# States times C in a two-branch block: decays put on C, channel-major by head pairs; output weights split earlier

## The chip, the cores and the metric

One core of a Trainium2 chip runs the whole kernel. The metric is device microseconds of one execution, as the median of 3 runs. TensorE (PE) multiplies into PSUM; its weight loads (PEld) are a queue of their own. VectorE (DVE), ScalarE (ACT) and GpSimd (POOL) work elementwise, each in the order of its own queue. SyncE (SP) and ACT issue the DMAs.

## What is computed

A block over 2048 latent tokens of 1024 channels (and 256 context tokens) has one input projection that feeds two mixers: box means on a grid, and a state-space scan in both directions with 16 heads of 64 channels in 4 groups. The scan goes in chunks of 128 tokens. For a chunk the output of a head is

```
y_diag = (C B^T masked, times decay) applied to x
y_off  = einsum('bclgn,bcgrpn,bclgr->bclgrp', C, h_start, exp(acum))
y      = y_diag + y_off          # forward, and the same backward; + d_skip * x
```

so `y_off` is the state at the chunk's border times C, scaled for each token and head by the exponential of the decay sum. y is gated, normed by group, joined with the pooled branch and multiplied by `w_out` (2048 x 1024); the kernel scales the rows of `w_out` (by `pool_scale` or the norm's weight) and its columns (by the gate `g_l`) once, ahead of time. Then come the residual and a last norm.

## The kernel before, in words

Channels lie on the partitions nearly everywhere. A projection's operands are split into a rounded part and a rest (`hi`, `lo`: a copy on ACT, a subtraction on POOL or DVE), and three matmuls of 512 columns make one product. The stages:

- **Convolution stage** (loop over 16 column tiles `ct`, lines 576 to 596). For each tile 4 blocks of 512 tokens are projected; for `ct` < 12 also the 256 context tokens (`hc`). A block's result is copied out of PSUM by ACT, goes through a convolution of three `scalar_tensor_tensor` on DVE (line 270) between two ACT operations, and is stored. Tiles 0 and 1 were spilled before; their convolutions (`recall`, the list `late`) come in blocks of `ct` 13 to 15. `gate_row` sums the gate row in `ct` 10 to 13 and stores it.
- **Upper projections** (lines 710 to 754): the upper half of the tokens through the gates and the pool branch, with the backward scan of states (`sweep`) between the matmuls. Here 8 of the 16 tiles of `w_out` are loaded, scaled (`rescale`, DVE reading the gate from two PSUM buffers `gb`) and stored to `s_wo`.
- **Lower projections and boxes** (lines 756 to 871): the lower half, and the box sums on DVE. `prepare(0)` to `prepare(3)` load a tile of `w_out`, scale it, copy the rounded part (ACT) and subtract the rest (POOL or DVE, line 851).
- **Ramp** (`RAMP`, lines 1207 to 1228): an order written out by hand for the first four steps, the last gate projections and `prepare(5)` to `prepare(8)`; `prepare(9)` to `(15)` follow.
- **Steps** (lines 1235 to 1253): 64 steps, one for each chunk c and group g of 4 heads. Every engine gets the operations of `ORDER` in that order; the number beside a name says which step it works on (-1 is the next step, 1 the one before). `carried` (line 911) multiplies C by both states (tokens on partitions, PSUM tile `yo`); `from_states` (line 941) scales the result by `ee_t` into `yt` on DVE; `outputs` (line 968) transposes the skip part and both halves of `yt` into PSUM tile `y` and adds the diagonal part, four matmuls of 64 output rows, the two heads of a pair on the two halves of the rows. `gate` (DVE) reads `y`. `state` (line 948) moves the forward state on, on POOL. `exponents`, `mix`, `mix2` (DVE), `shift`, `steps_mix`, `decay` (ACT) build the diagonal factor `m`; `norm1`, `norm2`, `diag`, `spread`, `scale` are the norm; `pool_lo`, `ssd_lo` are POOL's subtractions (line 960); `out` is the output product, 24 matmuls a step; `f0` to `f9` are the end of a chunk, spread over five steps.

Outside `RAMP` and the steps the framework orders each engine's queue itself. `aux` and `pp` are four PSUM buffers each.

Of the kernel before, what the change touches and what calls it, by code (L numbers as in the profile page):

```python
# [23 lines left out]
def hybrid_block(ctx, tc, d, out):  # L24
# [40 lines left out]
    s_gate = dram("s_gate", [P, 1024])  # L65
    s_wo = dram("s_wo", [8, P, 1024])
# [267 lines left out]
    wd = dp.tile([P, 8, P], F32R, tag="wd", name="wd")  # L334
# [168 lines left out]
    triL = const("triL", [P, P], d["triL"], pool=tabs)  # L503
    n4 = [P, 2, NC2, 16]
# [57 lines left out]
    def gate_row(k):  # L562

        wg = rpool.tile([P, 1024], F32, tag="wraw", name=f"wg{k}")
        nc.sync.dma_start(wg, d["w_ada"][k * P:(k + 1) * P, 2048:3072])
        if k == 0:
            nc.vector.tensor_scalar(gacc, wg, scol[:, k, 0:1], None, op0=ALU.mult)
        else:
            nc.vector.scalar_tensor_tensor(gacc, wg, scol[:, k, 0:1], gacc, op0=ALU.mult, op1=ALU.add)
        if k == 7:  # L570
            brow = rpool.tile([1, 1024], F32, tag="wraw", name="brow")
            nc.sync.dma_start(brow, d["b_g"])
            nc.vector.tensor_tensor(gacc[0:1, :], gacc[0:1, :], brow, op=ALU.add)
            nc.scalar.dma_start(s_gate, gacc)
# [4 lines left out]
    for ct in range(2, 16):  # L579
# [130 lines left out]
    with tc.tile_pool(name="sweepp", bufs=2) as bp, tc.tile_pool(name="evp", bufs=3) as ep:  # L710
# [10 lines left out]
        def rescale(raw, k):  # L721

            for j in range(2):
                js = raw[:, 512 * j:512 * j + 512]
                nc.vector.scalar_tensor_tensor(js, js, rowscale[:, k:k + 1], gb[j], op0=ALU.mult, op1=ALU.mult)

        upper = (2, 3)
        for j in range(8):
# [118 lines left out]

    def prep_lo(k, eng=None):
        wo = wout[k // 4][:, k % 4]
        eng = eng or (nc.gpsimd if k in (1,3,4,5,7,13,15) else nc.vector)  # L850
        eng.tensor_tensor(wo[:, 1, :], raws[k], wo[:, 0, :].bitcast(F32), op=ALU.subtract)  # L851

    def prepare(k):
        prep_load(k)
        prep_scale(k)
        prep_hi(k)
        prep_lo(k)
# [15 lines left out]
    class Step:  # L873
# [27 lines left out]

        def shift(s):
# [7 lines left out]

        def carried(s):

            g = s.g
            s.po = aux(f"yo{s.nm}")
            mm(s.po[:, 0:256], s.bc[:, 1, :], hst[:, g], True, True)
            mm(s.po[:, 256:512], s.bc[:, 1, :], s.st[:, 1, :], True, True)
# [210 lines left out]
    def z_tail(ps, j, b):  # L1127
# [12 lines left out]
        ("shift", -1, ('shift',)),  # L1140
# [10 lines left out]
        ("state", 0, ('state',)),  # L1151
        ("mask", -1, ('mask',)),
        ("outputs", 0, ('outputs',)),
        ("exponents", -1, ('exponents',)),
        ("steps_mix", -1, ('steps_mix',)),
        ("out01", 2, ('out', 0, 1)),
        ("decay", -1, ('decay',)),
        ("carried", -1, ('carried',)),
        ("f2", 0, None),
        ("pool_hi", 0, ('pool_hi',)),  # L1160
        ("gate", 0, ('gate',)),
        ("mix", -1, ('mix',)),
# [3 lines left out]
        ("squares", 0, ('squares',)),  # L1166
        ("square_sum", 0, ('square_sum',)),
# [35 lines left out]
    other = {f.__name__: f for f in (prep_load, prep_scale, prep_hi, prep_lo, z, zg, logs, work, more)}  # L1203
# [4 lines left out]
    0:load prep_load/5 1:load 0:scores 0:carried 0:shift 0:mask 0:exponents prep_scale/5 1:shift 0:steps_mix  # L1208
    prep_hi/5 logs 0:decay z/6/0 1:scores 1:carried zg/6/0 z/7/0 0:mix 0:from_states prep_load/6 
    0:mix2 1:mask 1:exponents 2:load prep_scale/6 1:steps_mix prep_hi/6 1:decay zg/7/0 2:scores 2:carried more  # L1210
    1:from_states 1:mix 0:outputs z/6/1 prep_lo/5 prep_load/7 0:load_pool prep_lo/6
    0:gate 2:mask prep_scale/7 1:mix2 prep_load/8 1:load_pool 0:squares 2:shift
    2:steps_mix 0:square_sum 2:exponents 1:outputs 0:norm_mm z/7/1 more work prep_hi/8 prep_hi/7 zg/6/1 prep_lo/8
    0:state prep_lo/7 3:load 2:from_states 1:gate 0:pool_hi 1:squares zg/7/1 logs 0:norm1 
    1:square_sum 0:norm2/0 1:pool_hi 2:decay 2:mix 0:pool_lo 1:pool_lo 3:scores 1:norm_mm 0:out/0/0
    0:out/0/1 1:norm1 0:norm2/1 0:norm2/2 0:norm2/3 0:diag 0:spread 2:mix2 3:mask 2:outputs 1:out/0/0 0:scale 3:carried 1:out/0/1
    0:ssd_hi 3:shift 2:state 0:ssd_lo 1:state 2:gate 3:steps_mix 2:squares 2:square_sum 3:exponents 2:norm_mm
    1:norm2/0
# [98 lines left out]
```

## Time and profile before

| | |
|---|---|
| median of 3 runs | 1695.05 us (1692.56 to 1697.28) |
| profiled execution | 1691.25 us; its span 1689.5 us |
| mean granted clock of TensorE | 0.983 |
| busy share of the span | PE 96%, PEld 77%, DVE 72%, ACT 45%, POOL 35% |
| HBM read, written | 207.28 MB, 93.62 MB |

The stages end at about 491 us (convolution), 823 (upper), 1057 (lower), 1154 (ramp), 1662 (steps). A line of a group reads: line of the kernel, engine, operation, out<-in, shapes, count | busy us, mean ns of one | idle time of the engine just before them, and who ended it. A matmul of plain 32-bit floats is two instructions in the trace. An instruction's time counts from when its engine took it up, so that it holds what it waits for inside the engine.

### The profile page before, as it was taken

The numbers are of one execution on the slowest core, as the hardware profiler recorded it, in microseconds if no ns is written. First come the engines' busy times: TensorE is split into PE (matmuls) and PEld (weight loads), VectorE is DVE, ScalarE is ACT, GpSimd is POOL, SyncE is SP. The second block draws the span as 40 slices with busy tenths as digits, with TensorE's granted clock in tenths as the row PEclk, the third lists the DMA queues.
The fourth block names the chain that finished last, engine by engine and source line by source line (L and its number), as shares of the span: only waits on it lengthen the run. The fifth ranks groups of instructions, "written<-read, shape, count | busy, mean of one in ns | idle before, by whom it ended". The sixth has DMA issues, their size and how long they took to land. (4 is left out here: it accounts for less than half of the span.)

```text
span 1689.5 us, 25001 instructions
## 1 busy us (share of the span) xinstructions
PE 1626.3 (96%) x7786; PEld 1306.6 (77%) x7786; DVE 1209.4 (72%) x2514; ACT 768.4 (45%) x1841; POOL 599.5 (35%) x667
## 2 busy tenths in 40 slices
PE   8889999999999999999999989869999999999997
PEld 6668888888887887787887868757888888888886
DVE  2575755566772888886199998547788888888885
ACT  5563453433453444443212122455565556555653
POOL 1231111111223667775433334323333333333331
PEclk9989999999999999999999999989999999999999
DMA  9823333466564678878624356675666667666762
GB/s 388 283 75 100 76 74 73 93 155 155 144 137 153 203 248 252 255 249 272 207 87 150 114 184 187 188 223 184 186 194 208 195 203 199 198 208 192 194 194 83
DMA packets 315543, 302.57 MB, mean 179 GB/s; under 512 B 132626, under 2 KB 244114, under 8 KB 312851
## 3 DMA queue, kind: packets, MB, share of 16 engines
q1 hardware_dynamic: 246594, 237.27, 48.9%
q10 hardware_dynamic: 68816, 63.71, 11.3%
q8 instruction: 61, 1.00, 0.2%
q14 instruction: 72, 0.58, 0.1%
HBM read 207.28 MB, written 93.62 MB: 178 GB/s over the span
## 5 line engine op out<-in xcount | busy, mean ns | idle before, releaser
L52 PE MATMUL px<-hm,w_x 128*128 128x512 f32 x1536 | 364.8, 397 | 2.7 <-ACT hm L205 2.4
L52 PEld LDWEIGHTS px<-hm,w_x 128*128 128x128 f32 x1536 | 288.0, 188 | 73.3 <-ACT hm L205 4.1
L52 PE MATMUL po<-wout,yp 128*128 128x512 f32 x768 | 213.0, 413 | 0.0
L52 PE MATMUL po<-wout,ys 128*128 128x512 f32 x768 | 211.0, 410 | 0.0
L52 PE MATMUL pz<-hm,w_z 128*128 128x512 f32 x768 | 188.9, 398 | 0.7 <-POOL w_z L220 0.7
L270 DVE SCALAR_TENSOR_TENSOR cacc<-u,conv_w,cacc 128x512 f32<-128x512 f32 x168 | 141.5, 854 | 66.3 <-POOL u L320 47.5
L52 PEld LDWEIGHTS pz<-hm,w_z 128*128 128x128 f32 x768 | 145.0, 189 | 36.0 <-POOL w_z L220 1.1
L52 PEld LDWEIGHTS po<-wout,yp 128*128 128x128 f32 x768 | 135.9, 190 | 34.7 <-issue 10.6
L52 PEld LDWEIGHTS po<-wout,ys 128*128 128x128 f32 x768 | 136.3, 190 | 23.7
L960 POOL TENSOR_TENSOR yp<-yl,yp 128x256 fp32r<-128x256 f32 x64 | 50.3, 786 | 229.2 <-ACT yp L956 220.8
L644 DVE TENSOR_TENSOR xw<-xt,w_t 128x256 f32<-128x256 f32 x144 | 99.3, 728 | 31.5 <-POOL xr L651 17.0
L651 POOL TENSOR_TENSOR xr<-xw,xh 128x512 fp32r<-128x512 f32 x72 | 99.7, 1387 | 27.4 <-ACT xh L649 27.4
L960 POOL TENSOR_TENSOR ys<-yg,ys 128x256 fp32r<-128x256 f32 x64 | 63.1, 986 | 116.9 <-ACT ys L956 66.6
L52 PE MATMUL ivationFunctionType.Copy<-hm,ivationFunctionType.Copy 128*128 128x512 f32 x384 | 97.7, 401 | 2.3 <-POOL ivationFunctionType.Copy L220 1.7
L52 PE MATMUL pv<-hm,w_v 128*128 128x512 f32 x384 | 92.9, 402 | 5.9 <-ACT zt L795 5.9
L52 PE MATMUL ivationFunctionType.Silu<-hm,ivationFunctionType.Silu 128*128 128x512 f32 x384 | 95.9, 396 | 0.0
L649 ACT CAST xh<-xw 128x512 fp32r<-128x512 f32 x72 | 44.7, 621 | 110.0 <-DVE xw L644 48.9
L52 PE MATMUL pzp<-hm,w_q 128*128 128x512 f32 x384 | 91.3, 396 | 1.2 <-ACT va L788 1.2
L52 PEld LDWEIGHTS pv<-hm,w_v 128*128 128x128 f32 x384 | 73.6, 192 | 24.1 <-ACT zt L795 6.3
L52 PEld LDWEIGHTS ivationFunctionType.Copy<-hm,ivationFunctionType.Copy 128*128 128x128 f32 x384 | 73.1, 191 | 20.5 <-POOL ivationFunctionType.Copy L220 2.1
L52 PEld LDWEIGHTS pzp<-hm,w_q 128*128 128x128 f32 x384 | 72.0, 188 | 19.2 <-ACT va L788 1.6
L904 ACT ACTIVATE e<-e,nrb_t 128x128 f32<-128x128 f32 x256 | 81.1, 388 | 12.2 <-DMA e<-s_rows 11.9
(269 smaller groups left out, 3046.3 us busy)
## 6 DMA issues: line engine op xcount, KB each, us to landing
e<-s_rows SPq DMA_DIRECT2D x128, 256.0 KB, 5.1
s_tok<-tkw ACTq DMA_DIRECT2D x64, 256.0 KB, 3.0
bc<-s_bc SPq DMA_DIRECT2D x64, 256.0 KB, 4.3
st<-s_tok SPq DMA_DIRECT2D x64, 256.0 KB, 5.5
xt<-s_xt SPq DMA_DIRECT2D x72, 128.0 KB, 3.4
ada<-in_w_ada_dram SPq DMA_DIRECT2D x8, 1024.0 KB, 15.7
wraw_x<-in_w_xbc_dram SPq DMA_DIRECT2D x16, 512.0 KB, 4.4
s_bc<-cacc ACTq DMA_DIRECT2D x32, 256.0 KB, 3.2
```

Source lines behind the costliest of these rows:

```text
L52: nc.tensor.matmul(o, l, r, start=start, stop=stop)
L270: nc.vector.scalar_tensor_tensor(acc, u[:, k:k + n], conv_w[:, ct, k:k + 1], acc, op0=ALU.mult, op1=ALU.add)
L644: nc.vector.tensor_tensor(xw[:, s], h4(xt), w_t[:, s, c, 4 * g:4 * g + 4].unsqueeze(2).broadcast_to([P, 4, 64]), op=ALU.mult)
L649: nc.scalar.copy(xh, xw)
L651: nc.gpsimd.tensor_tensor(xr, xw, xh.bitcast(F32), op=ALU.subtract)
L904: nc.scalar.activation(s.e2[:, h, :], s.e2[:, h, :], AF.Identity, bias=nrb_t[:, s.c, 4 * s.g + h:4 * s.g + h + 1])
L960: nc.gpsimd.tensor_tensor(y[:, 1], src, y[:, 0].bitcast(F32), op=ALU.subtract)
```

## The change

`carried` and `yt` are gone. `ends` (ACT, two Exp of 128x512) writes the exponentials of both decay sums into `cw`, one buffer; `from_states` multiplies them by C in place, the forward half on DVE, the backward half on POOL; `outputs` then multiplies the states by `cw` for each head, 64 output rows each, straight into `y`. `state` comes behind `outputs`, and `exponents`, `shift`, `decay` come later in `ORDER`. All 16 tiles of `w_out` are loaded, scaled, split and stored in the convolution stage, one in each block of `ct` 12 to 15, in the place of `hc`; later `prepare` only loads 1 MB. The recalls move to `ct` 7 to 11, the gate rows to `ct` 3 to 6.

```diff
-    s_wo = dram("s_wo", [8, P, 1024])
+    s_wo = dram("s_wo", [16, P, 2, 1024])
...
+            for j in range(2):
+                gb = aux(f"gb{j}")
+                mm(gb, allone, gacc[:, 512 * j:512 * j + 512], True, True)
+                nc.scalar.copy(gacc[:, 512 * j:512 * j + 512], gb)
+    def prep(k):
+        hi, lo = room[:, k % 2, 0, :], room[:, k % 2, 1, :]
+        raw = lo.bitcast(F32)
+        nc.sync.dma_start(raw, d["w_out"][k * P:(k + 1) * P, :])
+        leave()
+        nc.vector.scalar_tensor_tensor(raw, raw, rowscale[:, k:k + 1], gacc, op0=ALU.mult, op1=ALU.mult)
+        nc.scalar.copy(hi, raw)
+        nc.gpsimd.tensor_tensor(lo, raw, hi.bitcast(F32), op=ALU.subtract)
+        done.append((s_wo[k], room[:, k % 2]))
...
+    def leave():
+        for dst, w in done:
+            nc.sync.dma_start(dst, w.bitcast(F32))
+        done.clear()
...
-            if ct > 12 and late:
+            if ct >= 12:
+                prep(4 * ct - 48 + b)
+            elif ct > 6 and b % 2:
                 late.pop(0)()
-        if ct in (10, 11, 12, 13):
+        if 3 <= ct < 7:
             for k in range(2):
-                gate_row(2 * ct - 20 + k)
+                gate_row(2 * ct - 6 + k)
...
     def prepare(k):
-        prep_load(k)
-        prep_scale(k)
-        prep_hi(k)
-        prep_lo(k)
+        nc.sync.dma_start(wout[k // 4][:, k % 4].bitcast(F32), s_wo[k])
...
+        def ends(s):
+            s.cw = mp.tile([P, 2, 4, P], F32, tag="cw", bufs=1, name=f"cw{s.nm}")
+            nc.scalar.activation(s.cw[:, 0], s.e1, AF.Exp)
+            nc.scalar.activation(s.cw[:, 1], s.e2, AF.Exp)
...
         def from_states(s):
+            for k, eng in enumerate((nc.vector, nc.gpsimd)):
+                eng.tensor_tensor(s.cw[:, k], s.cw[:, k], s.bc[:, 1:2, :].broadcast_to([P, 4, P]), op=ALU.mult)
...
+                for k, (x, y) in enumerate(((hst[:, s.g], s.cw[:, 0]), (s.st[:, 1, :], s.cw[:, 1]),
+                                            (s.tk[:, 0, :], s.m))):
+                    for i in range(2):
+                        h = 2 * a + i
+                        nc.tensor.matmul(o[64 * i:64 * i + 64, :], x[:, 64 * h:64 * h + 64], y[:, h, :],
+                                         start=False, stop=k == 2, skip_group_check=True)
```

The order of the steps after, with the step in brackets: f1, norm1(1), out00(2), f5, mix2(0), ln(1), f6, from_states(0), radd(1), f8, scores(-1), rexp(1), ssd_lo(2), newt(1), diag(1), f0, out10(3), mask(-1), outputs(0), state(0), steps_mix(-1), out01(2), ends(-1), gate(0), mix(-1), squares(0), square_sum(0), shift(-1), f2, pool_hi(0), exponents(-1), f4, rb(1), scale(1), decay(-1), out11(3), f3, f7, norm_mm(0), f9, ssd_hi(1), pool_lo(0). `RAMP` is written anew in the same sense, without the preparation's arithmetic and with the last two gate results (`zg`) taken later.

## Rows read from the trace of the kernel before

**Rows 1.** busy time by stage: busy us of each engine (instructions), granted clock, DMA share, GB/s

```profile
147.40:402.00 254.60, 254.60 (x1214) 210.68 (x1213) 161.10 (x229) 106.06 (x163) 35.97 (x105) 1.00 0.45 94
402.00:491.60 89.60, 89.60 (x385) 72.13 (x385) 67.15 (x91) 44.87 (x70) 18.52 (x43) 1.00 0.62 148
491.60:823.00 331.40, 325.44 (x1373) 259.07 (x1373) 231.07 (x383) 136.59 (x295) 202.11 (x163) 0.99 0.72 229
1057.00:1154.00 97.00, 76.33 (x348) 59.99 (x346) 54.96 (x121) 49.22 (x103) 33.85 (x25) 0.89 0.67 202
1154.00:1662.00 508.00, 508.00 (x2833) 411.91 (x2831) 413.94 (x1449) 300.25 (x965) 182.63 (x228) 1.00 0.66 194
```

**Rows 2.** PE in order of time, one step of the last stage: start us, us, instructions

```profile
1401.60 0.38 PE L52 MATMUL cb<-bc 128*128 128x128 f32 x2
1403.22 0.27 PE L973 MATMUL y<-ident,tk 128*128 128x128 f32 x1
1403.97 0.66 PE L979 MATMUL y<-m,tk 128*64 128x128 f32 x8
1404.56 1.67 PE L52 MATMUL po<-wout,yp 128*128 128x512 f32 x6
1406.06 0.59 PE L52 MATMUL yo<-hst,bc 128*128 128x256 f32 x2
1406.93 0.38 PE L52 MATMUL n<-dg,allone 128*128 128x128 f32 x2
1410.18 0.38 PE L52 MATMUL cb<-bc 128*128 128x128 f32 x2
```

**Rows 3.** weight loads of PE in order of time, the same step

```profile
1403.97 0.42 PEld L979 LDWEIGHTS y<-m,tk 128*64 128x64 f32 x8 [0.17 <-issue]
```

**Rows 4.** groups of DVE, 1154 to 1662: count, busy us, mean ns, idle before by releaser

```profile
L935 DVE SCALAR_TENSOR_TENSOR m<-cbl,dt_t,m 128x128 f32<-128x128 f32 x236 | 72.8, 369 | 0.0
L899 DVE SCALAR_TENSOR_TENSOR e<-e,af_t,e 128x128 f32<-128x128 f32 x235 | 66.4, 343 | 0.0
L939 DVE TENSOR_TENSOR m<-m,e 128x512 f32<-128x512 f32 x59 | 46.9, 794 | 0.0
L123 DVE SCALAR_TENSOR_TENSOR rv<-rv,rr 128x1 f32<-128x1 f32 x59 | 17.9, 303 | 23.7 <-ACT rr L120 23.7
```

**Rows 5.** DVE and POOL in order of time, two short stretches

```profile
1137.65 3.22 DVE L899 SCALAR_TENSOR_TENSOR e<-e,af_t,e 128x128 f32<-128x128 f32 x4
1137.70 2.50 POOL L851 TENSOR_TENSOR wout<-wor,wout 128x1024 fp32r<-128x1024 f32 x1 [3.18 <-ACT wout L846]
...
1417.78 0.68 DVE L939 TENSOR_TENSOR m<-m,e 128x512 f32<-128x512 f32 x1
1418.38 0.68 DVE L944 TENSOR_TENSOR yt<-yo,ee_t 128x512 f32<-128x512 f32 x1
1419.04 0.61 DVE L123 SCALAR_TENSOR_TENSOR rvf<-rvf,rrf 128x1 f32<-128x1 f32 x1
1417.86 1.20 POOL L960 TENSOR_TENSOR ys<-yg,ys 128x256 fp32r<-128x256 f32 x1 [1.76 <-ACT ys L956]
1419.02 0.61 POOL L951 TENSOR_TENSOR hst<-hst,dec_t 128x256 f32<-128x256 f32 x1
```

**Rows 6.** groups of POOL, 491.6 to 823

```profile
L651 POOL TENSOR_TENSOR xr<-xw,xh 128x512 fp32r<-128x512 f32 x72 | 99.7, 1387 | 27.4 <-ACT xh L649 27.4
```

**Rows 7.** groups of ACT, 1154 to 1662

```profile
L930 ACT ACTIVATE e<-e 128x512 f32<-128x512 f32 x59 | 37.3, 632 | 0.2
```

**Rows 8.** groups of DVE and POOL, 402 to 491.6

```profile
L270 DVE SCALAR_TENSOR_TENSOR cacc<-ur,conv_w,cacc 128x512 f32<-128x512 f32 x22 | 16.4, 744 | 5.4 <-ACT cacc L268 5.2
L569 DVE SCALAR_TENSOR_TENSOR gacc<-wg,scol,gacc 128x1024 f32<-128x1024 f32 x2 | 2.6, 1286 | 4.8 <-DMA wg<-in_w_ada_dram 4.8
L220 POOL TENSOR_TENSOR w_x<-wraw_x,w_x 128x1024 fp32r<-128x1024 f32 x3 | 7.7, 2577 | 1.6 <-ACT w_x L219 1.6
```

**Rows 9.** groups of PE, 823 to 1154: count, busy us, mean ns, idle before by releaser

```profile
L52 PE MATMUL pv<-hm,w_v 128*128 128x512 f32 x384 | 92.9, 402 | 5.9 <-ACT zt L795 5.9
```

More of the change, by code (lines that the diff above doesn't have):

```diff
@@ L333, in hybrid_block @@
     dt_raw = const("dt_raw", [P, NC2, 32], pool=dp)
-    wd = dp.tile([P, 8, P], F32R, tag="wd", name="wd")
+    wd = sp.tile([P, 8, P], F32R, tag="wd", bufs=1, name="wd")
     ctxt = Tokens(hc, 256, d["ctxT"], 1, "c", wpool.tile([P, 8, 256], F32, tag="w", name="xc"))
@@ L587, in hybrid_block @@
             col.context_out()
+        elif ct == 12:
+            room = dp.tile([P, 2, 8, 256], F32R, tag="hc", name="wos")
+            room = room.rearrange("p a b c -> p (a b c)").rearrange("p (i h n) -> p i h n", i=2, h=2)
         for b in range(4):
@@ L909, in scores @@
             mm(s.pc[:, 0:P], s.bc[:, 0, :], s.bc[:, 1, :], True, True)
[L911 to L916, printed above, removed]
         def mask(s):
@@ L1150, in hybrid_block @@
         ("out10", 3, ('out', 1, 0)),
-        ("state", 0, ('state',)),
         ("mask", -1, ('mask',)),
         ("outputs", 0, ('outputs',)),
-        ("exponents", -1, ('exponents',)),
+        ("state", 0, ('state',)),
         ("steps_mix", -1, ('steps_mix',)),
         ("out01", 2, ('out', 0, 1)),
-        ("decay", -1, ('decay',)),
-        ("carried", -1, ('carried',)),
+        ("ends", -1, ('ends',)),
+        ("gate", 0, ('gate',)),
+        ("mix", -1, ('mix',)),
+        ("squares", 0, ('squares',)),
+        ("square_sum", 0, ('square_sum',)),
+        ("shift", -1, ('shift',)),
         ("f2", 0, None),
         ("pool_hi", 0, ('pool_hi',)),
-        ("gate", 0, ('gate',)),
-        ("mix", -1, ('mix',)),
+        ("exponents", -1, ('exponents',)),
         ("f4", 0, None),
@@ L1165, in hybrid_block @@
         ("scale", 1, ('scale',)),
-        ("squares", 0, ('squares',)),
-        ("square_sum", 0, ('square_sum',)),
+        ("decay", -1, ('decay',)),
         ("out11", 3, ('out', 1, 1)),
@@ L1202, in hybrid_block @@
     kp = None
-    other = {f.__name__: f for f in (prep_load, prep_scale, prep_hi, prep_lo, z, zg, logs, work, more)}
+    other = {f.__name__: f for f in (prepare, z, zg, logs, work, more)}
     RAMP = """
[L1208 to L1214, printed above, removed]
+    0:load prepare/5 1:load 0:scores 0:ends 0:shift 0:mask 0:exponents 0:steps_mix
+    logs 0:decay z/6/0 1:scores zg/6/0 z/7/0 0:mix 0:from_states prepare/6
+    0:mix2 1:mask 2:load 2:scores more
+    0:outputs 0:state 0:load_pool 1:steps_mix 1:ends 0:gate 1:shift 1:exponents 1:decay zg/7/0 logs 1:mix 1:from_states
+    z/6/1 prepare/7 1:mix2 0:squares prepare/8 1:load_pool
+    0:square_sum 1:outputs 1:state 0:norm_mm z/7/1 more work 2:mask 2:steps_mix 2:ends
+    1:gate 3:load 2:shift 2:exponents 2:from_states 0:pool_hi 1:squares 0:norm1
     1:square_sum 0:norm2/0 1:pool_hi 2:decay 2:mix 0:pool_lo 1:pool_lo 3:scores 1:norm_mm 0:out/0/0
-    0:out/0/1 1:norm1 0:norm2/1 0:norm2/2 0:norm2/3 0:diag 0:spread 2:mix2 3:mask 2:outputs 1:out/0/0 0:scale 3:carried 1:out/0/1
-    0:ssd_hi 3:shift 2:state 0:ssd_lo 1:state 2:gate 3:steps_mix 2:squares 2:square_sum 3:exponents 2:norm_mm
-    1:norm2/0
+    0:out/0/1 1:norm1 0:norm2/1 0:norm2/2 0:norm2/3 0:diag 0:spread 2:mix2 3:mask 2:outputs 2:state 1:out/0/0 0:scale 1:out/0/1
+    0:ssd_hi 3:steps_mix 3:ends 0:ssd_lo 2:gate 3:shift 2:squares 2:square_sum 3:exponents zg/6/1 zg/7/1 2:norm_mm
+    logs 1:norm2/0
     """
```

53 lines of the change are left out of this document (7 added, 46 removed).

## The prediction

> **What bounds the kernel now.** I read the table of busy times by stage first [rows 1]. In the steps, from 1154 to 1662 us, PE is busy 508.0 of 508.0 us: every microsecond that PE gives or takes there counts, and 59 steps pass, 508 / 59 = 8.61 us each. DVE is busy 413.94 us, 7.02 a step; ACT 300.25, 5.09; POOL 182.63, 3.10. PE rests only ahead of the steps: 331.4 - 325.4 = 6 us in the upper projections, 97.0 - 76.3 = 20.7 in the ramp, where the granted clock was 0.89. The two stretches of the convolution stage have no idle PE.
>
> Then one step on PE in order of time [rows 2]. From one `cb` to the next it is 8.58 us. `yo`, the product that goes, holds PE from 1406.06 to 1406.93, 0.87 us. The six transposes into `y` hold it from 1403.22 to 1403.97, 0.75; the eight rows of diagonal matmuls, which are 4 matmuls of two instructions each, from 1403.97 to 1404.56, 0.59. Their 8 weight loads took 0.42 us in that stretch [rows 3].
>
> Last, DVE and POOL beside one another. In the groups of DVE [rows 4], the product `m*e` takes 794 ns in the mean, and in one place 0.68 [rows 5]. The pairs of rows [rows 5] say why: four `e` operations on SBUF took 3.22 us beside a POOL subtraction of 2.50 that began with them, where four such groups take 4 x 0.343 = 1.37 in the mean of the steps [rows 4]. A 128x1 operation took 0.61 beside a POOL `hst` of 0.61, and POOL's `ys` took 1.20 behind `m`, where the other POOL operation of its size took 0.61. So **a DVE operation with two tensors from SBUF and one of POOL's don't run at the same time**: each waits for the other's end. `yt`, at 1418.38, ran its 0.68 while POOL's `ys` ran on: it reads PSUM.
>
> **The change, part by part.**
>
> PE in a step. `carried` goes: -0.87. Four of six transposes go: the six cost 0.75 with some 0.1 of switching, about 0.109 each, so -0.44. Eight pairs' worth of work comes: 16 matmuls of 64 output rows, two heads side by side. The 4 diagonal ones are 2 pairs, in two instructions (passes) each, 4 pair passes in 0.59; with 0.15 for the switch I put 0.44 / 4 = 0.11 on a pass. The states' 8 matmuls make 4 pairs, 8 passes: +0.87. Sum -0.44: **PE alone would go to 8.17 us a step**, -0.44 x 59 = -26 us.
> That two heads share the time is my reading of the rows: one behind the other the 8 instructions would have cost 0.87, and took 0.59.
> The Trainium skill ("TensorE: Matmul & The Clock Gate", Part 3, The mechanism) says that a weight load overlaps running matmuls only where the row group differs, and the two heads of a pair differ in columns alone. By it 16 loads of 0.42 / 8 us, an estimate of +0.84, would stand in the open and PE's step would be 9.0. The trace is against it: 0.42 of loads and 0.44 of passes fit into 0.59.
>
> DVE in a step. `yt` (0.68) goes, the forward half of the new `from_states` comes: the same 128x512 elements at the 0.68 of an undisturbed `m*e` [rows 5]. By busy time nothing changes. But `yt` ran beside POOL, and the new halves can't: both read two tensors from SBUF. POOL's half has the size of the 128x512 subtraction, 1.39 us [rows 6]; from below 1.3, since that mean has waits in it.
> - In `ORDER`, POOL's half is the first thing behind `pool_lo`, and `cw` is there since the middle of the step before. It starts at the head of the step, and `mix2` on DVE meets it: 0 to 1.39, I take 1.0.
> - `ssd_lo` (0.73: `ys` of 1.20 less the 0.47 from its start to the end of `m`'s turn, where `yt` began at 1418.38 with some 0.05 of gap) stands ahead of DVE's half: 0 to 0.73, I take 0.6.
> - `state` (two operations of 0.61 or more), now behind `outputs`, falls into `mix`: 0 to 1.2, I take 0.6.
> - Today's 7.02 holds such waits already: 0.11 on each `m*e` and on some small operations, some 0.45, to be taken off.
> That is +1.75.
> The Trainium skill ("SBUF — State Buffer", the ports of the engines) calls the shared pair a lock held for the full instruction. By it alone `mix2` waits for up to all of POOL's half, and the step would be 0.4 longer than my sum; the `e` row above, 3.22 beside 2.50, agrees.
>
> Handoffs in DVE's ring. `outputs` now waits for both halves, `gate` for `outputs`; between them DVE has only `mask` and Newton's steps, so I put 0.2 on it. The chain add, Exp on ACT, Newton keeps its 23.7 / 59 = 0.40 [rows 4]. `squares` now stands behind two Exps of 0.63 [rows 7] on ACT, and `square_sum` on DVE behind it: +0.3. Sum 0.9.
> **DVE's ring: 7.02 + 1.75 + 0.9 = 9.67, say 9.6 us a step.** It is above PE's 8.17, so it sets the step: 9.6 - 8.6 = +1.0, x 59 = **+59 us**. With the lower ends of the waits (0.5 in all) it is 8.4, with the upper ones (3.3 - 0.45) 10.8. A second count leans the same way: POOL's 3.10 + 1.35, and DVE's `m`, `e`, `m*e`, `rv` and the new half, (72.8 + 66.4 + 46.9 + 17.9) / 59 + 0.68 = 4.14 [rows 4], may not overlap: 8.59 with today's waits in it.
>
> Added waits. `ends` has one buffer, so ACT waits with it for `outputs` of the step before; behind it on ACT stand `squares`, `shift`, `pool_hi`, `decay`, and for these wait `square_sum` on DVE, `norm_mm` on PE and `exponents`. ACT has 5.09 + 2 x 0.63 = 6.4 us of work, so this costs place, not time, and is in the 0.3. `aux` loses a buffer's use per step (three tiles for four): no cost.
>
> Convolution stage, `ct` 12 to 15, 22.4 us a tile. To each tile come 4 scalings of 1.29 on DVE, 4 subtractions of 2.58 on POOL [rows 8], 4 copies on ACT, 4 loads of 0.5 MB and 4 stores of 1 MB. What may not overlap: DVE's 12 x 0.74 of convolution and 4 x 1.29, POOL's 5 x 2.58: 27 us against 22.4. DVE thus falls 4 x 4.5 = 18 us behind, less what four PSUM buffers let stand. The recalls that leave (10, over three tiles) give 10 x 3 x 0.74 = 22 us back. I take **+5**, from 0 to +20. On SP the stores wait for POOL, and the next tile's weights stand behind them; they are asked for a tile ahead, which hides a wait of a few us.
> Recalls and gate rows go to `ct` 3 to 11, where DVE works 161 of 254.6 us [rows 1]: 0, hidden by PE; bare it would be the 22 us of the recalls.
>
> Upper and lower projections. 16 scalings of 512, 8 loads, 8 stores and two PSUM buffers' holding leave: -2 of the 6 idle. In the lower half, `prepare(0)` scaled on DVE ahead of the last `z`; PE waited 5.9 us for ACT's `zt` in `pv` [rows 9] and came back at a low clock. I take -5, from -7 to 0.
>
> Ramp. Copies, scalings and subtractions of four tiles leave DVE, ACT and POOL, `carried` leaves PE; the 2.50 beside 3.22 [rows 5] is one of these. Against it, four loads are 1 MB, not 0.5: 2 MB more over 97 us, 20 GB/s on top of 202 [rows 1]; and seven of 1 MB follow at once ahead of the steps' loads, 7 MB at 202 / 0.67 = 300 GB/s or 23 us. They are asked for while the ramp runs. I take **-10**, from -20 to +10.
>
> Sum outside the steps: 5 - 2 - 5 - 10 = -12 (-29 to +30). **In all +59 - 12 = +47.** The profiled execution, 1691.25 us (span 1689.5), would become 1738; the median of the runs lies 3.8 above it, so 1695.05 + 47 = 1742.
>
> **The rivals.**
> 1. *PE stays the bound* (ends faster). If POOL's half finds a place where DVE reads PSUM (`gate`, `mask`, `scale`, the `rv` from `n`), the waits stay near today's and DVE's ring is 7.0 + 0.9 + 0.1, under PE's 8.17. Then -26 - 12 = -38: 1657. For it: DVE has 1.6 us of slack now, and nothing in `ORDER` forbids the place. Against it: `cw` is early and POOL free, so the half starts where `mix2` stands.
> 2. *The waits are half as large.* Ring 8.7, +6 - 12: 1689. It is the even point: the change is slower only where the step is above 8.8.
> 3. *The preparation starves PE as well* (slower still): in `ct` 12 to 15 the 18 us appear in full and the loads queue behind the stores, with the steps at 9.6 and no gain in the ramp: 1695 + 59 + 18 = 1772.
> 4. *The change does not do what it says*: the 64-row matmuls of different heads run one behind the other, and PE's step is 8.17 + 0.87 = 9.0, with DVE at 8.4: +0.4 x 59 - 12 = +12, 1707.
>
> **How the numbers follow.** A measurement of this kernel tells about 0.3%, 5 us, from no change. Chances: the forecast 0.57 (its own range, steps of 9.0 to 10.3: 1706 to 1783), rival 1 0.26, rival 2 0.09 (0.03 faster, 0.05 same, 0.01 slower), rival 3 0.05, rival 4 0.03. I stay under 0.6 because a place of POOL's half half a step later turns the sign. Faster 0.29, same 0.05, slower 0.66. The range has to hold both signs: 1650 to 1785; left out are steps over 10.3 and rival 1 with the best ramp.
>
> **What would show it.** Right: from `cb` to `cb` 9.6 us in PE's order of time; PE idle ahead of `y` or `norm_mm`, ended by DVE's or POOL's `cw` or by ACT; `m*e` over 1 us in the mean, beside a POOL operation on `cw` of about 1.35; DVE busy over 8.5 us a step. PE's own work 8.2 a step, 12 pair passes in some 1.4 us. In the convolution stage a few us of idle PE from 402 on; no 5.9 at `pv`; less than 20.7 idle in the ramp. Wrong: PE busy all through the steps at 8.2, with `m*e` near 0.7, is rival 1; pair passes of 0.22 are rival 4.

## The result: slower, 1758.8 us, and the profile after

The changed kernel takes 1758.76 us in the median (1758.2 to 1761.53) against 1695.29 of the kernel before in the same measurement: a ratio of 1.0395, 95% interval [1.0372, 1.0418]. That is +63.5 us where +47 was forecast. The profiled execution took 1761.53 us, span 1759.7.

The table of busy times by stage of the changed kernel (stretch, its us; busy us of PE, PEld, DVE, ACT, POOL; granted clock; DMA share; GB/s):

```profile
402.00:510.00 108.00, 93.93 (x392) 75.25 (x391) 83.11 (x79) 50.50 (x72) 46.78 (x50) 0.92 0.78 248
510.00:837.40 327.40, 321.67 (x1369) 258.80 (x1369) 238.74 (x368) 140.89 (x299) 211.64 (x168) 0.99 0.69 221
837.40:1063.00 225.60, 224.58 (x962) 180.23 (x961) 189.21 (x63) 42.42 (x60) 82.36 (x52) 1.00 0.49 161
1160.70:1720.30 559.60, 496.46 (x3249) 397.82 (x3248) 485.46 (x1426) 350.50 (x1070) 271.60 (x287) 0.97 0.61 177
```

Beside [rows 1]: the end of the convolution stage moves from 491.6 to 510.0 (+18.4). The upper projections take 327.4 for 331.4 (-4), the lower ones 225.6 for 233.7 (-8.1). The ramp, up to the scores of step 5, takes 97.7 for 95.1 (+2.6). The last row reaches from the scores of step 5 to those of step 63, 58 steps: 559.6 us, where the kernel before took 499.6 with PE busy throughout. That is 9.65 us a step for 8.61, +60 us in all. In a step DVE is busy 485.46 / 58 = 8.37 us and rests 1.28; in the kernel before it was 7.03 and 1.58. PE now rests 63 us in the steps, most of it ahead of `outputs`, for DVE's half (what PE waited for, us in total, times, longest):

```profile
PE y L965 <- DVE cw L931: 57.1, 48, 2.1
```

So the loss is in two places, the steps and the convolution stage; two smaller gains stand against it. What DVE does in the steps, by groups (count | busy us, mean ns | idle us before, by releaser):

```profile
L926 DVE TENSOR_TENSOR m<-m,e 128x512 f32<-128x512 f32 x59 | 84.9, 1439 | 1.6
L887 DVE SCALAR_TENSOR_TENSOR e<-e,af_t,e 128x128 f32<-128x128 f32 x232 | 80.8, 397 | 0.0
L922 DVE SCALAR_TENSOR_TENSOR m<-cbl,dt_t,m 128x128 f32<-128x128 f32 x232 | 80.0, 402 | 0.2
L931 DVE TENSOR_TENSOR cw<-cw,bc 128x512 f32<-128x512 f32 x58 | 56.0, 965 | 0.0
L972 DVE TENSOR_TENSOR yg<-y,bc 128x256 f32<-128x256 f32 x58 | 24.4, 420 | 23.1 <-PE y L965 23.1
L982 DVE TENSOR_TENSOR dec_t<-dec_t 128x128 f32<-128x128 f32 x29 | 8.4, 290 | 7.6 <-ACT dec_t L978 7.6
L982 DVE TENSOR_TENSOR af_t<-af_t 128x128 f32<-128x128 f32 x29 | 8.4, 290 | 21.7 <-ACT af_t L978 21.7
```

`m*e` has gone from 794 to 1439 ns [rows 4] and DVE's own half of `from_states` takes 965 where 680 is its time alone. The small sums `dec_t` and `af_t` are `square_sum`: DVE rests (7.6 + 21.7) / 58 = 0.5 us a step ahead of them for ACT's squares, and 23.1 / 58 = 0.4 ahead of `gate` for PE's `y`. One step in order of time, DVE, ACT and POOL:

```profile
1444.18 0.28 DVE L908 TENSOR_TENSOR cbl<-cb,triL 128x128 f32<-128x128 f32 x1
1444.38 0.41 DVE L972 TENSOR_TENSOR yg<-y,bc 128x256 f32<-128x256 f32 x1
1444.82 1.23 DVE L922 SCALAR_TENSOR_TENSOR m<-cbl,dt_t,m 128x128 f32<-128x128 f32 x4
1447.05 0.29 DVE L982 TENSOR_TENSOR af_t<-af_t 128x128 f32<-128x128 f32 x1 [1.00 <-ACT af_t L978]
1447.34 1.23 DVE L887 SCALAR_TENSOR_TENSOR e<-e,af_t,e 128x128 f32<-128x128 f32 x4
...
1449.64 1.46 DVE L926 TENSOR_TENSOR m<-m,e 128x512 f32<-128x512 f32 x1
...
1444.40 1.27 ACT L914 ACTIVATE m<-cbl,dt_t 128x128 f32<-128x128 f32 x4
1445.57 0.62 ACT L893 ACTIVATE cw<-e 128x512 f32<-128x512 f32 x1
1446.09 0.62 ACT L894 ACTIVATE cw<-e 128x512 f32<-128x512 f32 x1
1446.61 0.40 ACT L978 ACTIVATE af_t<-yg 128x256 f32<-128x256 f32 x1
1446.92 1.26 ACT L898 ACTIVATE e<-e,nrb_t 128x128 f32<-128x128 f32 x4
...
1449.26 1.30 POOL L931 TENSOR_TENSOR cw<-cw,bc 128x512 f32<-128x512 f32 x1
1450.51 1.17 POOL L945 TENSOR_TENSOR ys<-yg,ys 128x256 fp32r<-128x256 f32 x1
```

Two things are to be seen. POOL's half begins at 1449.26, and `m*e`, taken up at 1449.64, ends at 1451.10: it stood until POOL was done at about 1450.5 and ran its 0.6 then, while POOL's `ys`, taken up at 1450.51, waited in its turn (1.17 for 0.73). And between the mask (to 1444.46) and the first `shift` (1446.92) ACT has a row of work one behind the other: `steps_mix`, the two Exps of `ends`, the squares. DVE, which needs squares and shift, has `gate` and `mix` to do meanwhile and then rests 1.00 us. From the mask to the end of the first shift that row is about 2.8 us.

### The profile page after: what moved, and what is told of

Same layout as the page of the kernel before. It is cut to its first block, busy times and chain, and to the rows that moved or that the text cites. A ratio compares the mean times of both kernels' runs of the same rounds, so it can differ in the third digit from the quotient of the medians.

```text
span 1759.7 us, 26086 instructions
## 1 busy us (share of the span) xinstructions
PE 1620.5 (92%) x8298; PEld 1299.8 (74%) x8298; DVE 1305.0 (74%) x2489; ACT 833.8 (47%) x1975; POOL 725.5 (41%) x740
## 3 DMA queue, kind: packets, MB, share of 16 engines
q10 hardware_dynamic: 67520, 58.99, 10.1%
## 4 chain that ended last, share of the span: by engine, by line
PE 43%; DVE 28%; ACT 11%; DMA 10%; issue 4%; SPq 2%; POOL 2%; ACTq 0%; DVEq 0%; POOLq 0%
PE px L52 9%; PE pz L52 6%; PE ivationFunctionType.Copy L52 5%; DVE m L926 5%; DVE e L887 4%; PE ivationFunctionType.Silu L52 4%; PE pv L52 4%; DVE cacc L269 3%; ACT m L914 3%; PE st L52 3%; PE pzp L52 3%; DVE cw L931 2%; PE po L52 2%; PE y L965 2%; DVE bx L830 2%
## 5 line engine op out<-in xcount | busy, mean ns | idle before, releaser
L52 PE MATMUL px<-hm,w_x 128*128 128x512 f32 x1536 | 367.7, 399 | 16.8 <-ACT u L314 14.1
L52 PE MATMUL po<-wout,yp 128*128 128x512 f32 x768 | 221.8, 426 | 0.0
L269 DVE SCALAR_TENSOR_TENSOR cacc<-u,conv_w,cacc 128x512 f32<-128x512 f32 x168 | 162.3, 981 | 44.1 <-POOL u L319 26.5
L52 PEld LDWEIGHTS po<-wout,yp 128*128 128x128 f32 x768 | 142.8, 199 | 37.5 <-issue 11.9
L965 PE MATMUL y<-cw,hst 128*64 128x128 f32 x512 | 55.1, 295 | 59.2 <-DVE cw L931 59.1
L670 DVE TENSOR_TENSOR xw<-xt,w_t 128x256 f32<-128x256 f32 x144 | 92.8, 684 | 19.1 <-POOL xr L677 15.0
L931 POOL TENSOR_TENSOR cw<-cw,bc 128x512 f32<-128x512 f32 x64 | 95.8, 1497 | 10.1 <-DMA st<-s_tok 5.6
L887 DVE SCALAR_TENSOR_TENSOR e<-e,af_t,e 128x128 f32<-128x128 f32 x256 | 89.6, 399 | 4.7 <-ACT e L898 4.7
L926 DVE TENSOR_TENSOR m<-m,e 128x512 f32<-128x512 f32 x64 | 90.2, 1410 | 1.6
L922 DVE SCALAR_TENSOR_TENSOR m<-cbl,dt_t,m 128x128 f32<-128x128 f32 x256 | 89.2, 406 | 2.5 <-ACT m L914 2.3
```

Source lines behind the costliest of these rows:

```text
L52: nc.tensor.matmul(o, l, r, start=start, stop=stop)
L269: nc.vector.scalar_tensor_tensor(acc, u[:, k:k + n], conv_w[:, ct, k:k + 1], acc, op0=ALU.mult, op1=ALU.add)
L670: nc.vector.tensor_tensor(xw[:, s], h4(xt), w_t[:, s, c, 4 * g:4 * g + 4].unsqueeze(2).broadcast_to([P, 4, 64]), op=ALU.mult)
L887: nc.vector.scalar_tensor_tensor(s.e1[:, h, :], s.e1[:, h, :], af_t[:, 0, s.c, i:i + 1], s.e2[:, h, :], op0=ALU.subtract, op1=ALU.min)
L922: nc.vector.scalar_tensor_tensor(s.m[:, h, :], s.cbl[:, 1, :], dt_t[:, 1, s.c, i:i + 1], s.m[:, h, :], op0=ALU.mult, op1=ALU.add)
L926: nc.vector.tensor_tensor(s.m, s.m, s.e1, op=ALU.mult)
```

## The experiments

Three theories. **The port**: POOL's half and DVE's operations on SBUF wait for each other. **The row on ACT**: with one buffer for `cw` the Exps can't come before `outputs`, so they stand between mask and squares. **The preparation**: in the convolution stage it meets the recalls. The step is the mean from the scores of step 5 to those of step 63. The first of these run unevenly, and differently in each kernel. From step 13 to step 61 the same pattern comes back with each chunk of four, more or less, and there the changed kernel takes 9.69 us a step and the kernel before 8.62. A ratio is to the kernel before, run beside it; the changed kernel's is 1.0395.

### The parts alone

`steps_alone` is the kernel before with the new steps, their order and their ramp, which holds the old preparation. Against the changed kernel's ramp:

```diff
-    0:load prepare/5 1:load 0:scores 0:ends 0:shift 0:mask 0:exponents 0:steps_mix
+    0:load prep_load/5 1:load 0:scores prep_scale/5 0:ends 0:shift 0:mask 0:exponents 0:steps_mix prep_hi/5
...
```

> The changed steps with the preparation of the kernel before (its ramp carries that preparation's work). If the loss is in the steps, as the changed kernel's trace has it (9.65 us a step against 8.61, 58 steps, +60 us), this kernel is at 1695 + 60 = 1755, give or take 8 for its ramp. If the preparation disturbs the steps, for instance by leaving DMA queues or clocks behind, the steps come back toward 8.6 and it is near 1700 to 1720.

Measured: 1.0370 [1.0348, 1.0391], 1750.65 us against 1687.62, +63; the step 9.62. The loss is in the steps.

`prep_alone` is the changed kernel with the old steps, order and ramp, the ramp only loading:

```diff
-            for k, eng in enumerate((nc.vector, nc.gpsimd)):
-                eng.tensor_tensor(s.cw[:, k], s.cw[:, k], s.bc[:, 1:2, :].broadcast_to([P, 4, P]), op=ALU.mult)
+            s.yt = mp.tile([P, 2, 256], F32, tag="yt", name=f"yt{nm}")
...
+        ("carried", -1, ('carried',)),
```

> The steps of the kernel before with the new preparation. From the two traces by stage: convolution stage +18.4 us, upper projections -4, lower -8, ramp 0 to -10, steps 0: between 1691 and 1702, about no change. If the forecast's -12 outside the steps held apart from the changed ramp, 1683.

Measured: 1.0006 [0.9994, 1.0018]; the step 8.61. The new preparation alone costs nothing and brings nothing: PE waits 10.1 us for ACT's `u` in the convolution stage, and the later stages give it back. The -12 outside the steps was not there.

### The port

`no_pool_half`:

```diff
-            for k, eng in enumerate((nc.vector, nc.gpsimd)):
+            for k, eng in enumerate((nc.vector,)):
```

> The changed kernel without POOL's half of from_states: the backward states are multiplied by the exponentials alone, C is left out of them. Port theory: the step falls by about 1.25, to 8.4, since nothing but POOL's 1.25 leaves; the time to 1759 - 1.2 x 60 = 1687. Rival (late outputs and two more exponentials on ACT make the step): the step stays above 9.3 and the time above 1738.

Measured: 1.0160 [1.0143, 1.0177], 1714.7 us; the step 8.93, where 8.4 was expected. POOL's 1.3 us cost 0.72 us a step, and 0.32 of the loss of 1.04 stays; from step 13 to 61 the step is 9.02, which is 0.67 less, and 0.40 of 1.07 stays. So the port is a large part and not the whole. Its groups of DVE over the same 58 steps:

```profile
L931 DVE TENSOR_TENSOR cw<-cw,bc 128x512 f32<-128x512 f32 x58 | 49.5, 854 | 0.0
L926 DVE TENSOR_TENSOR m<-m,e 128x512 f32<-128x512 f32 x58 | 39.8, 687 | 1.6
L982 DVE TENSOR_TENSOR dec_t<-dec_t 128x128 f32<-128x128 f32 x29 | 8.5, 292 | 17.5 <-ACT dec_t L978 17.3
L982 DVE TENSOR_TENSOR af_t<-af_t 128x128 f32<-128x128 f32 x29 | 8.5, 292 | 25.1 <-ACT af_t L978 25.0
```

`m*e` is back at 687 ns, so its 1439 was waiting for POOL. What is left is plain: the rest ahead of `square_sum` has grown to 42.6 / 58 = 0.73 us a step.

`both_dve` gives POOL's half to DVE:

```diff
-            for k, eng in enumerate((nc.vector, nc.gpsimd)):
+            for k, eng in enumerate((nc.vector, nc.vector)):
```

> The changed kernel with both halves of from_states on DVE and none on POOL; same results. Theory of the shared port: POOL's half holds DVE for about 1.25 us a step (m*e 1.44 in the mean against 0.79, DVE's half 0.97 against 0.68, the rest on e, m and small operations), DVE's second half costs 0.6: the step falls by 0.4 to 0.65 to 9.0 to 9.25, and the time by 25 to 38 to 1721 to 1734. Rival, DVE's ring is simply full and no port is in it: DVE gets 0.6 more work, the step grows to 10.2 and the time to 1795. Rival, the chain from the gate through the outputs sets the step: no change within 5.

Measured: 1.0315 [1.0298, 1.0332]; the step 9.36, a fall of 0.29 where 0.4 to 0.65 was expected. The sign is the port's: DVE got work and the step became shorter. The size is smaller; DVE still rests 1.15 us a step.

`c_psum_early` lets PE copy C to PSUM, where DVE's half reads it, ahead of `mix2`:

```diff
+            mm(s.pc[:, P:2 * P], ident, s.bc[:, 1, :], True, True)
...
-            for k, eng in enumerate((nc.vector, nc.gpsimd)):
+            for k, eng, cc in ((0, nc.vector, s.pc[:, P:2 * P].unsqueeze(1)), (1, nc.gpsimd, s.bc[:, 1:2, :])):
```

> The changed kernel with C copied to PSUM by PE (one more product of 128 columns, +0.22 us of PE a step), DVE's half of from_states reading it there, and standing ahead of mix2, beside POOL's half. Port theory: DVE's half then does not wait (0.97 to 0.68) and covers part of POOL's 1.25, so m*e falls from 1.44 to about 0.9: the step falls by 0.5 to 0.8 to 8.85 to 9.15, the time by 29 to 47. Rival, the port does not care where DVE reads: no change, or +0.2 from PE.

Measured: 1.0307 [1.0292, 1.0323]; the step 9.36, below the changed kernel but not down to 9.15. Its groups of DVE:

```profile
L927 DVE TENSOR_TENSOR m<-m,e 128x512 f32<-128x512 f32 x58 | 56.5, 974 | 0.0
L932 DVE TENSOR_TENSOR cw<-cw,cb 128x512 f32<-128x512 f32 x58 | 39.3, 677 | 0.0
L117 DVE TENSOR_TENSOR rr<-rt 128x1 f32<-128x1 f32 x58 | 32.4, 558 | 0.0
L127 DVE TENSOR_TENSOR rr<-rr,rv 128x1 f32<-128x1 f32 x58 | 28.9, 498 | 2.0
```

The half that reads PSUM takes 677 ns: it waits for nobody, as `yt` did in [rows 5]. In one place POOL's half and DVE's stand side by side:

```profile
1415.62 2.27 POOL L932 TENSOR_TENSOR cw<-cw,bc 128x512 f32<-128x512 f32 x1
1416.98 0.68 DVE L932 TENSOR_TENSOR cw<-cw,cb 128x512 f32<-128x512 f32 x1
```

Part of the waiting has moved on to two operations on 128x1, with both inputs in SBUF, which took 0.15 and 0.20 in the kernel before: other operations beside POOL's pay now.

### The row on ACT

`squares_first` takes `gate` and `squares` ahead of `ends` in the order:

```diff
-        ("ends", -1, ('ends',)),
         ("gate", 0, ('gate',)),
+        ("squares", 0, ('squares',)),
+        ("ends", -1, ('ends',)),
         ("mix", -1, ('mix',)),
-        ("squares", 0, ('squares',)),
```

> The changed kernel with gate and squares ahead of the two Exps of ends in the order of the steps; the same results. Without POOL's half DVE still rested 1.3 us a step, 0.85 to 1.0 of it ahead of square_sum, for squares behind steps_mix and the two Exps on ACT (about 1.0 together). Theory that this handoff is half of the loss that the port does not explain: the step falls by 0.2 to 0.5 to 9.2 to 9.45, the time by 12 to 28. Rival, the loop through the one buffer of cw (outputs, two Exps, shift, exponents, Exp, m*e, cw, outputs) sets the step, and squares only give their place on ACT to it: the Exps come 0.3 later, the step is the same or up to 0.3 longer.

Measured: 1.0459 [1.0443, 1.0474], slower than the changed kernel; the step 9.76. The rival held. The waits of DVE, 1160.7 to 1670 (us in total, times, longest):

```profile
DVE e L887 <- ACT e L898: 29.4, 40, 1.2
DVE yg L972 <- PE y L965: 23.7, 39, 1.7
```

The rest ahead of `square_sum` is gone, and one ahead of `exponents`, for `shift`, stands in its place: the whole row is what DVE waits for, not one member of it.

`best` has this order, C in PSUM and the recalls from `ct` 4 on:

```diff
-            elif ct > 6 and b % 2:
+            elif ct > 3 and b % 2 and late:
```

> Both of the two before, and the recalls three tiles earlier (from ct 4 on). If the port and the squares' handoff add up: step 8.5 to 8.8, with PE's own 8.4 near; convolution stage without its idle 14 us: 1759 - 50 to 65 - 14 = 1680 to 1695, about as fast as the kernel before. If the loop through cw holds: step 9.2, 1720.

Measured: 1.0381 [1.0364, 1.0399]; the step 9.72, above both values expected, against 9.36 for C in PSUM alone: the squares' place spoils it.

To shorten the row the Exps must leave it, and that wants a second buffer of `cw`. `two_cw` has it and goes back to the old order, with `ends` at the head of the step:

```diff
-            s.cw = mp.tile([P, 2, 4, P], F32, tag="cw", bufs=1, name=f"cw{s.nm}")
+            k = 4 * s.c + s.g
+            s.cw = (wp2 if k > 7 and k % 2 else mp).tile([P, 2, 4, P], F32, tag="cw", bufs=1, name=f"cw{s.nm}")
...
+        ("exponents", -1, ('exponents',)),
...
+        ("decay", -1, ('decay',)),
```

> The changed kernel with a second buffer for cw, which lets ends go to the head of the step and the rest of the order stand as in the kernel before (shift, exponents and decay early; state behind outputs). Theory that with one buffer mask, steps_mix, the two Exps, squares and shift stand in one row on ACT (3 us) ahead of exponents, while DVE has 1.75 us of work, and that this is the second half of the loss: DVE's rest falls from 1.3 to about 0.5 a step, the port's waits stay, the step falls to 8.7 to 9.0, the time by 38 to 55. Rival, the port alone: step 9.5 to 9.65, no change over 8.

Measured: 1.0702 [1.0682, 1.0722], far off; the step 10.41. PE in order of time, from the step that costs most:

```profile
1418.50 1.66 PE L52 MATMUL po<-wout,yp 128*128 128x512 f32 x6
...
1425.64 0.56 PE L52 MATMUL n<-mcol,dec_t 128*128 128x1 f32 x2 [3.21 <-DVE dec_t L983]
1426.06 2.91 PE L52 MATMUL po<-wout,yp 128*128 128x512 f32 x6
```

With `exponents` ahead of `gate` and `state` meeting `mix`, `square_sum` comes so late that PE stands 3.21 us before the norm product, with the output products queued behind it. Afterwards the same six output matmuls took 2.91 us, not 1.66; over the steps the granted clock was 0.91 in the mean, some of the time at 1.2 GHz and not 2.4. The experiment changed the order in more places than the theory spoke of and decides nothing on the row.

`two_cw_psum` adds C in PSUM and the early recalls to it:

```diff
+        ("from_states", 0, ('from_states',)),
         ("mix2", 0, ('mix2',)),
...
-        ("from_states", 0, ('from_states',)),
```

> Both causes taken away: second buffer for cw with the old order, C in PSUM for DVE's half, which stands ahead of mix2 beside POOL's half, and the recalls from ct 4 on. If port waits (8.36 to 8.1 of DVE) and the row on ACT are the whole loss, DVE is busy about 8.0 with 0.4 of rest and PE has 8.4 of its own: step 8.4 to 8.6 and a time of 0.985 to 0.996 of the kernel before. If a third cause is left (loads, the outputs' latency): step above 8.8, 1.01 or more.

Measured: 1.0606 [1.0583, 1.0629]; the step 10.25, with the same waits of PE for `square_sum`, up to 3.1 us.

`ends_head` keeps the changed order and moves the Exps alone:

```diff
+        ("ends", -1, ('ends',)),
         ("norm1", 1, ('norm1',)),
...
-        ("ends", -1, ('ends',)),
         ("gate", 0, ('gate',)),
```

> The changed kernel with a second buffer for cw and the two Exps of ends at the head of the step; all else in the changed order. The kernel with the whole old order lost by PE's norm product, which waited up to 3.2 us behind exponents and scale; here that part of the order stays. Theory of the row on ACT (steps_mix, two Exps, squares, shift between mask and exponents, 3 us, with one buffer and the Exps in it): the row is 1.04 shorter, DVE's rest of 1.3 a step falls to 0.3 to 0.6, the step to 8.7 to 9.1, the time by 30 to 55. Rival, the row is not what DVE waits for, or the port's waits move in where the rest was: the step stays above 9.4, the time within 12 of the changed kernel's ratio 1.0395.

Measured: 1.0245 [1.0215, 1.0274]; the step 9.12, and 9.00 from step 13 to 61. The waits of DVE, 1160.7 to 1670:

```profile
DVE rr L117 <- ACT rt L115: 20.8, 17, 2.7
DVE rv L122 <- ACT rr L119: 11.6, 43, 0.3
DVE yg L973 <- PE y L966: 9.4, 26, 0.4
```

No wait for squares or shift is left. Taking the Exps out of the row on ACT is worth 0.53 us a step, 0.69 from step 13 on. That is not DVE's rest alone: it falls from 1.28 to 0.92, and DVE's busy time from 8.37 to 8.21. `m*e` is still 1.16 us in the mean (1200 to 1650 us): much of the port's share stands. From step 13 on the port (0.67) and the row (0.69) are worth nearly the same, and together more than the whole loss of 1.07, so they overlap, and which is the larger is not shown.

### The preparation

In the changed kernel PE rests once in the convolution stage, for 14.1 us. The waits around it (PE from 402 to 510 us, ACT and SP from about 402 to 446):

```profile
PE px L52 <- ACT u L314: 14.1, 1, 14.1
ACT cacc L271 <- DVE cacc L269: 14.7, 5, 6.0
ACT cacc L267 <- DMA ur<-s_raw: 6.6, 1, 6.6
SPq L257 <- DVE ur L253: 8.9, 2, 5.5
```

ACT, which empties PE's PSUM buffers, stood 6.6 us for the load of a recall. That load, asked for at 412.7 us, stood on SP behind stores; the first of them waited 5.5 us for DVE's transpose, and the twelve took SP from 406.1 to 412.6. ACT's longer waits, 14.7 us, were for DVE's convolutions, which were late themselves: 1.17 us in the mean from 402 to 510 us, for 0.88 in the kernel before, beside POOL's subtractions of 2.5.

`prep_recall_early` is `prep_alone` with the recalls from `ct` 4 on (the line shown for `best`).

> The steps of the kernel before, the new preparation, and the recalls three tiles earlier. In the trace PE rests 10.5 to 14 us in ct 12 to 13, where ACT waits 6.6 us for a recall's load that stands on SP behind stores which wait for DVE. Theory that recalls beside the preparation make that stall: it goes and the time falls by 10 to 14, to 0.993 of the kernel before. Rival, the port alone makes it (subtractions of 2.4 to 2.8 on POOL beside DVE's convolutions): it stays, or moves by under 4 us.

Measured: 0.9957 [0.9942, 0.9972], 1680.84 us: the stall is gone, with the subtractions still on POOL and DVE's convolutions still at 1.13 us. So the stall needs the recalls; whether it needs POOL's port too was not tried. PE has 99.5 busy of the 100 us from 402 on; 10.8 us of waiting appear in the upper projections instead:

```profile
PE ivationFunctionType.Silu L52 <- ACT ivationFunctionType.Silu L218: 8.1, 1, 8.1
PE ivationFunctionType.Silu L52 <- POOL ivationFunctionType.Silu L219: 2.7, 1, 2.7
```

`prep_early_dve` takes the preparation's subtraction from POOL:

```diff
-        nc.gpsimd.tensor_tensor(lo, raw, hi.bitcast(F32), op=ALU.subtract)
+        nc.vector.tensor_tensor(lo, raw, hi.bitcast(F32), op=ALU.subtract)
```

> The steps of the kernel before, the new preparation with early recalls, and its subtraction on DVE, not on POOL. With early recalls PE has no rest in the convolution stage, but 11 us in the upper projections, 8.1 of it for weights that ACT rounds late while the preparation's last tiles run on. If the port is what makes the preparation late (2.4 us on POOL for 1.2 on DVE), it ends earlier and 5 to 8 of the 11 go: 0.991 to 0.993 of the kernel before. If SP's row of loads and stores makes it late, no change: 0.9957.

Measured: 0.9877 [0.9862, 0.9891], 1666.15 us against 1687.15. **This version beats both kernels**, the one before by 1.2%. By stage (convolution from 402 us on, upper, lower, ramp):

```profile
402.00:494.10 92.10, 92.10 (x396) 74.15 (x395) 71.68 (x73) 45.66 (x62) 21.70 (x35) 1.00 0.85 280
494.10:813.90 319.80, 318.66 (x1370) 256.83 (x1369) 228.72 (x366) 137.57 (x294) 201.09 (x161) 1.00 0.67 217
813.90:1039.50 225.60, 224.56 (x962) 180.24 (x961) 189.28 (x63) 42.31 (x60) 82.64 (x52) 1.00 0.48 162
1039.50:1128.70 89.20, 74.71 (x336) 58.61 (x335) 32.38 (x97) 36.14 (x86) 20.50 (x19) 0.90 0.83 286
```

PE is busy 92.1 of 92.1 and 318.7 of 319.8 us. The gain does not lie in the convolution stage, which is 2.5 us longer than in the kernel before, but behind it: -11.7 in the upper projections (331.5), -8.1 in the lower ones (233.7), -5.9 in the ramp (95.1). The subtraction took 2.5 us on POOL and 1.2 on DVE, so it is both shorter and out of POOL's port; the run does not part the two. Some waiting beside POOL is left: DVE's convolutions take 0.95 us in the mean, and POOL still splits the weights. The gain over `prep_recall_early` is more than the 5 to 8 us expected of it.

## Why the forecast was right, point by point

- **The steps: right in the sum, off in its parts.** The forecast was 9.6 us a step and +59; measured 9.65 and +60 over 58 steps. Its terms: the port's waits were put at +1.75, and DVE's busy time grew by 8.37 - 7.03 = 1.34. The handoffs were put at 0.9, and the rest is 1.28. The two errors nearly cancel, which is luck; of the signs named for the steps one failed, DVE's busy time, 8.37 where over 8.5 was asked for. The mis-sized term of the handoffs is "`squares` now stands behind two Exps ... +0.3": with 0.5 a step, and 0.73 once the port's share is out, it was the two Exps together with `steps_mix` ahead of them. I had counted only what stands ahead of the squares, not where the mask starts the row. The forecast did name the wait of `ends` for `outputs` and who stands behind it, and then said that it "costs place, not time": `ends_head`, which takes that wait away, is 0.53 us a step shorter. The low end of the range, "0.5 in all" and 8.4, does not follow from its terms, whose low ends are all 0; no result hangs on it.
- **What `mix2` meets.** 1.0 of wait was taken; `m*e` grew by 1.44 - 0.79 = 0.65. The two other waits were put too high as well: DVE's half grew by 0.28 where 0.6 was taken, and `mix` by 0.14 with `exponents` by 0.27, where 0.6 was taken for `mix` alone. POOL's half starts while DVE is at the small one-input operations of the norm (1449.26 against 1449.64), so part of it is covered. The Trainium skill ("SBUF — State Buffer", SBUF: two separate sides) has whoever starts first hold the shared ports for the whole instruction, which would have had up to all of POOL's half in that wait and a step 0.4 longer. That a wait lasts to the end of POOL's instruction agrees with the trace (1.46 beside 1.30); that DVE waits from its start does not follow.
- **PE alone at 8.17: right.** In the first steps of `no_pool_half` PE is the bound, five steps of 8.14 us:

```profile
1158.00:1198.70 40.70, 40.70 (x282) 33.40 (x281) 35.23 (x109) 28.14 (x87) 15.30 (x20) 1.00 0.68 196
```

  With `ends_head` PE is busy 478.0 of 529.2 us, 8.24 a step. (In the changed kernel it is 8.56, at a granted clock of 0.97.) The heads' pairs run side by side: 24 instructions from 1442.24 to 1443.70, 12 pair passes of 0.12, while the weight loads run:

```profile
1442.24 0.44 PE L965 MATMUL y<-cw,hst 128*64 128x128 f32 x4
1443.38 0.39 PE L965 MATMUL y<-m,tk 128*64 128x128 f32 x4
1443.70 1.67 PE L52 MATMUL po<-wout,yp 128*128 128x512 f32 x6
1442.24 0.20 PEld L965 LDWEIGHTS y<-cw,hst 128*64 128x64 f32 x4 [0.35 <-DVE cw L931]
1443.28 0.25 PEld L965 LDWEIGHTS y<-m,tk 128*64 128x64 f32 x4
```

  The loads of this stretch, six groups of 0.20 to 0.25 us, sum to 1.45 us and fit beside the matmuls. The rule that they overlap only across row groups (the Trainium skill, "TensorE: Matmul & The Clock Gate", Part 3) does not describe this trace, as [rows 2, 3] had it.
- **Outside the steps: -12 forecast, some +9 measured** (+18.4 - 4 - 8.1 + 2.6), and this is nearly all of the miss: 21 of the 23 us by which the profiled spans miss the +47. (The two profiled spans lie 70.2 us apart and the medians 63.5; the stages are told by the spans.) The projections did somewhat better than forecast: -4 for -2, and -8.1 for -5, beyond the -7 of its range. The convolution stage was put at +5 on the argument that four PSUM buffers let DVE's lag stand and that the recalls leave, "from 0 to +20". That +18.4 lies near the 18 us of lag is chance. It is one rest of PE of 14.1 us and a lower clock behind it (0.92 for the stretch), and with the recalls three tiles earlier, the subtractions still on POOL, the stage takes 93.2 us from 402 on, 3.6 more than before, much as forecast. The failed step is "the recalls that leave": the trace has them beside the first tiles of the preparation, and `prep_recall_early` shows that they made the stall. ACT empties PE's PSUM buffers in its queue, and it stood behind a recall's load.
- **The ramp: -10 forecast, +2.6 measured.** With the old steps and the new preparation (`prep_alone`) the stretch from the lower projections' end to step 5 is shorter, 87.6 against 95.1 us. In the changed kernel PE rests 24.7 us there, not less than 20.7, most of it in two waits for one kind of load (PE, 1063 to 1160.7 us):

```profile
PE cb L52 <- DMA bc<-s_bc: 16.0, 2, 15.1
```

  The long one is for the load that holds B and C of step 3. SP asked for it at 1120.3 us, behind two loads of the pooled branch that held SP from 1104.1 to 1115.4 and behind four 1 MB tiles of `w_out`; it was there at 1132.7. `prep_alone` asked for it at 1112.2, ahead of its last four tiles, and has 1.3 us of this wait, `steps_alone` none. The forecast had counted the larger loads and then put them at nothing, since they "are asked for while the ramp runs".
- **The rivals.** PE as the bound (1657) needed a place for POOL's half beside DVE's reads of PSUM. `c_psum_early` made such a place, and the step fell only to 9.36, with DVE resting (27.7 + 28.4) / 58 = 0.97 us a step ahead of `square_sum`: the row on ACT still stood. The step of 9.65 is against rival 2 (8.7), the pair passes of 0.12 against rival 4 (0.22). Rival 3, at 0.05, came nearer than the forecast: steps at 9.6, the 18 us in the convolution stage in full, no gain in the ramp, 1772 against 1758.8 measured and 1742 forecast; it left out what the projections give back. The forecast was right on the steps and wrong on the preparation.

Not tried: the port's half and the Exps' place taken away together with nothing else. From step 13 on the single effects, 0.67 and 0.69, would sum to a step of 8.33, below the 8.62 of the kernel before; that they add is not shown, and `c_psum_early` warns that waits move.

## What to carry to other kernels

Before a half of the work is given to POOL, ask which DVE operations with two SBUF tensors run beside it: 1.3 us there cost some 0.7 us a step on an engine that had 1.6 us of rest. A single buffer between two engines fixes a place in a third engine's queue; write down the row of work that then stands between two operations of the bounding engine, from its first release to its last, and not the last member alone. Work that is moved into a stage with no idle PE is not hidden by PSUM buffers if the engine that empties them can stand behind a load; here the moved preparation paid 0.4% with the recalls out of its way and 1.2% with its subtraction off POOL as well.

## What the runs showed that was not expected

- DVE with PSUM on one side ran at 677 ns beside POOL's 2.27 us, and the waits it no longer had came back in part on operations of 128x1 (0.15 to 0.56 us). A small operation next to one of POOL's can wait as long as a large one.
- A lower clock of PE hardly lengthened the changed kernel. From step 13 to step 60 a chunk of four steps takes 38.6 to 38.7 us where the granted clock is full throughout (three chunks). In the nine others the first step has a granted clock of 0.86, part of it at the lower level, and takes 11.8 to 11.9 us; the four together take 38.2 or 38.3 us in five of them, with the next step down to 8.1, and 39.2 to 39.8 in the other four, 38.8 in the mean. A slow step of PE is made up in the next ones, in part or in whole, which agrees with DVE's ring setting the pace.
- A kernel with an extra buffer was the slowest: `two_cw` has a second `cw` and takes 1806.64 us, for its order; with the Exps alone moved, in the changed order, the same buffer is worth 1.5% (1.0245 for 1.0395).
